# RWKV half pairs of a hybrid step: where the chunk decay is applied, which engine masks and copies, and in which order small products are issued

## The chip, the cores and the metric

The kernel runs on one core of a Trainium2 chip, as one program. A core has five engines that work side by side and wait for each other through semaphores: TensorE (PE in the profile: matrix products into PSUM), VectorE (DVE), ScalarE (ACT), GpSimd (POOL) and SyncE (SP, which issues the DMAs here). PSUM, into which products are written, is used here in eight banks of 512 fp32 columns. The metric is the device time of the execution in microseconds (us); less is better. Three executions of the kernel before took 3572.85, 3575.87 and 3577.72 us.

## The reference

One layer is computed for 512 latent tokens and 128 context tokens with shared weights: an adaLN modulation, one input projection, attention (8 heads) beside a bidirectional RWKV-7 mixer (16 heads of 64), an output projection with a post-norm, and a SwiGLU feed-forward part with a post-norm. The change works on the mixer, and on one small product of attention. The mixer's core is a scan in each direction:

```python
    def step(S, inp):
        r_t, w_t, k_t, v_t, kk_t, a_t = inp
        sa = jnp.einsum("bhvk,bhk->bhv", S, -kk_t)
        S = S * w_t[:, :, None, :] + sa[..., None] * (kk_t * a_t)[:, :, None, :] + v_t[..., None] * k_t[:, :, None, :]
        return S, jnp.einsum("bhvk,bhk->bhv", S, r_t)
```

So a state S of 64 x 64 for each head is decayed by w, corrected along kk, and extended by v k; the output is S r. In attention a score is the product of query and key without position, plus the product of their rotary parts.

## The kernel before

**Tiling.** The 640 tokens lie along the free axis, features on the 128 partitions. Two heads make a pair: head h of a pair stands on partitions 64h to 64h + 63. A pair is worked in two half pairs, j = 0 and 1; in each, the forward direction (d = 0) takes one half of the tokens and the backward direction (d = 1) the other. Tokens go in chunks of 64 (C), five for each direction, so 10 chunks a half pair (NCH), and there are 8 x 2 = 16 half pairs.

**A half pair.** `rwkv_decays` forms decay and learning rate by low-rank products (a full product with the rounded weights, and one with 64 rows for the remainder) and, by a scan, the decay inside each chunk (`dd`, whose last column is kept as `dc`, the decay of the whole chunk). `rwkv_prep` writes the scaled keys `nk` (10 chunks x 128 columns) and the scaled queries `pr`, one tile for each head. `rwkv_grams` forms nk x pr of each chunk and head, a product with 64 rows, 128 output partitions and 128 columns; EG groups the chunks 4, 4 and 2, and each group and head takes one PSUM bank. From the bank ACT copies one part to `mab`, DVE writes one part times a causal mask back into `pr`, and DVE writes the last part times the mask into `mrb`. `inverse` inverts the triangular matrices of all chunks: four copies of `mab` by ACT into a diagonal layout `nd`, a row of small DVE operations, and then products of 32 x 32. Beside it `rwkv_turned` turns values into `sv` (ACT) and `zv` (DVE) and transposes `nk` into `bk`.

**The chain.** `rwkv_chain` then walks the five chunks, both directions and heads together. A step forms x from the state (`m<-sv,pr`, hop "x"), multiplies it by the inverse (`m<-xs,uf`, hop "s") into `zv`, and forms the product pn for the new state (`m<-zv,bk`, hop "y"). On DVE, `sd` = pn + old state, and the new state is `sd` times `dc`. `outputs` adds, for each direction in turn, the state's part (`m<-pr,sv`) and the values' part (`m<-mrb,zv`) of y; both directions share a bank. Then comes hop "p".

**The order of the work.** PE's instructions stand in an order written out when the program is built: class `Jobs` keeps a set of generators with ranks and a planned clock (`Tensor.now`), and always goes on with the ready one of the lowest rank. A generator yields a hop, the planned time in us until it is ready again, from `HOPS` (the first table while the input projection runs, the second while attention does). RWKV has rank 0, its side work (decays of the next half, `rwkv_post`, `rwkv_bonus`) 1, the modulation weights 2, attention 3, the input projection 4. While RWKV waits for a hop, a lower job fills PE. PE then runs the list strictly in order. On the other engines the framework orders the instructions itself, by dependencies and a simulated timeline. It also keeps two engines from reading one PSUM bank at once.

**PSUM.** `mps()` gives one of three banks (tag "m") in turn, to grams, chain, decays, inverse and some of attention; `acc()` gives two tiles of two banks to the projections and scores; `xps()` gives one bank.

**Attention.** Operands are split into a rounded high part and a remainder. `product` sums five products a score; the last has the 64 rows of the head's rotary query part (`qx`) and the rotary key's remainder `krl`. Keys, values and the rotary key parts share 12 slots (`kslot`, N_K).

In the profile the tile names tell these apart: `m<-pr,nk` grams, `m<-xl,lw` the low-rank remainder, `m<-cst,v` the value transposes, `m<-cst,nk` the key transposes, `acc<-krl,qx` the rotary remainder, `acc<-xh,whi` and its like the projections. A form such as 64*128 gives the rows and columns of the array that a product uses. L112 is the line of the helper that issues products, L226 that of the elementwise helper.

## Time and profile before

| what | us |
|---|---|
| median of three executions | 3575.87 |
| the profiled execution, its own time | 3577.47 |
| its span, first to last instruction | 3575.70 |
| start, up to the first half pair's grams | 285 |
| input projection and RWKV | 895 |
| attention and the rest of RWKV | 368 |
| output projection and feed-forward | 2028 |

The stages were told apart by the names of the products that PE runs. The mean granted TensorE clock was 0.959 of full speed. The span is 1.8 us shorter than the execution's own time, which has the launch and the end around it. A row of the order of time gives the start, the time to the end of the last of its instructions, engine, line, operation, tiles, shapes and count; a row of grouped instructions gives busy time and mean, then the engine's idle time just before them and what ended it. [...]

### The profile page before, as it was taken

How to read it: one execution, taken by the hardware profiler on the slowest of the kernel's cores; microseconds unless marked ns; L12 is line 12 of the kernel's file. 1: busy time of each engine (PE TensorE's matmuls, PEld its weight loads, DVE VectorE, ACT ScalarE, POOL GpSimd, SP SyncE). 2: the span in 40 equal slices, each digit the busy share in tenths (PEclk: the TensorE clock that was granted, in tenths of full speed). 3: DMA queues.
4: the chain of work that ended last, by engine and by line, in shares of the span. 5: the costliest groups of instructions: out<-in, count | busy, mean ns of one | idle time of the engine just before them, and what ended most of it. 6: DMA issues, size and time to landing. Idle time of an engine off the chain costs nothing. (4 is left out here: it accounts for less than half of the span.)

```text
span 3575.7 us, 71303 instructions
## 1 busy us (share of the span) xinstructions
PE 3391.9 (95%) x27538; PEld 3032.9 (85%) x27538; DVE 2627.2 (73%) x4721; ACT 1460.2 (41%) x2987; POOL 994.1 (28%) x944
## 2 busy tenths in 40 slices
PE   8979999999999999999979999999999989999987
PEld 4667776777887778889979999999999989999987
DVE  1355676666676776667788988888888868778898
ACT  1143333333444444444453444444444434334334
POOL 0021111111111212111164544444444432222245
PEclk9988999999998999999989999999999999999997
DMA  8653444444112111066534443444433468666743
GB/s 296 236 171 125 142 152 138 155 153 137 60 58 86 37 41 37 18 215 196 154 113 136 165 129 128 133 138 138 136 124 127 143 227 296 234 245 213 257 126 106
DMA packets 289716, 529.05 MB, mean 148 GB/s; under 512 B 31008, under 2 KB 83680, under 8 KB 289376
## 3 DMA queue, kind: packets, MB, share of 16 engines
q1 hardware_dynamic: 289376, 524.49, 44.6%
q8 instruction: 216, 3.54, 0.4%
q14 instruction: 124, 1.02, 0.1%
HBM read 429.65 MB, written 93.09 MB: 146 GB/s over the span
## 5 line engine op out<-in xcount | busy, mean ns | idle before, releaser
L226 DVE TENSOR_TENSOR ql<-raw,qh 128x512 fp32r<-128x512 f32 (+1 forms) x1136 | 932.2, 834 | 282.9 <-ACT qh L1290 270.4
L1290 ACT CAST qh<-raw 128x512 fp32r<-128x512 f32 (+1 forms) x1136 | 661.0, 589 | 880.5 <-PE b L112 658.2
L226 POOL TENSOR_TENSOR raw<-raw,raw 128x512 f32<-128x512 f32 (+1 forms) x288 | 405.6, 1412 | 824.0 <-DVE ql L226 577.7
L112 PE MATMUL b<-t,qh 128*128 128x320 f32 x2816 | 626.9, 310 | 7.9 <-ACT qh L1290 6.8
L112 PE MATMUL b<-op,qh 128*128 128x320 f32 x2464 | 555.0, 318 | 26.0 <-DMA op<-hd 12.7
L112 PEld LDWEIGHTS b<-t,qh 128*128 128x128 f32 x2816 | 473.7, 189 | 9.1 <-ACT qh L1290 7.5
L112 PE MATMUL b<-p,qh 128*128 128x320 f32 x2112 | 468.2, 310 | 0.7 <-ACT qh L1290 0.7
L112 PEld LDWEIGHTS b<-op,qh 128*128 128x128 f32 x2464 | 422.2, 194 | 37.0 <-DMA op<-hd 15.7
L112 PE MATMUL b<-t,ql 128*128 128x320 f32 x1408 | 436.9, 311 | 5.8 <-DVE ql L226 5.8
L112 PE MATMUL b<-op,ql 128*128 128x320 f32 x1232 | 378.0, 319 | 17.0 <-DVE ql L226 17.0
L112 PEld LDWEIGHTS b<-p,qh 128*128 128x128 f32 x2112 | 354.3, 188 | 1.3 <-ACT qh L1290 1.2
L112 PE MATMUL b<-p,ql 128*128 128x320 f32 x1056 | 327.9, 311 | 7.0 <-DVE ql L226 7.0
L112 PEld LDWEIGHTS b<-t,ql 128*128 128x128 f32 x1408 | 265.2, 188 | 8.7 <-DVE ql L226 8.6
L112 PEld LDWEIGHTS b<-op,ql 128*128 128x128 f32 x1232 | 235.2, 194 | 25.4 <-DVE ql L226 25.0
L226 DVE TENSOR_TENSOR raw<-raw,raw 128x512 f32<-128x512 f32 (+1 forms) x288 | 246.4, 866 | 11.5 <-POOL raw L226 5.8
L112 PE MATMUL acc<-xh,whi 128*128 128x320 f32 x928 | 239.7, 341 | 0.3 <-DVE vS L1145 0.2
L112 PE MATMUL acc<-xh,wlo 128*128 128x320 f32 x928 | 235.6, 336 | 0.8 <-DVE wlo L226 0.8
L112 PE MATMUL b<-mh,qh 128*128 128x320 f32 x1024 | 229.6, 313 | 7.0 <-ACT qh L1290 7.0
L112 PE MATMUL acc<-xl,whi 128*128 128x320 f32 x928 | 236.2, 337 | 0.0
L112 PEld LDWEIGHTS b<-p,ql 128*128 128x128 f32 x1056 | 198.9, 188 | 9.4 <-DVE ql L226 9.4
L263 ACT CAST whi<-raw 128x512 fp32r<-128x512 f32 (+1 forms) x156 | 95.0, 609 | 257.1 <-PE acc L112 167.4
L226 DVE TENSOR_TENSOR wlo<-raw,whi 128x512 fp32r<-128x512 f32 (+1 forms) x156 | 107.3, 688 | 111.4 <-ACT whi L263 79.5
(328 smaller groups left out, 5847.5 us busy)
## 6 DMA issues: line engine op xcount, KB each, us to landing
wm<-in_w_mod_dram SPq DMA_DIRECT2D x64, 1024.0 KB, 5.4
op<-hd SPq DMA_DIRECT2D x154, 320.0 KB, 6.0
raw<-in_w_gate_dram SPq DMA_DIRECT2D x188, 256.0 KB, 2.7
raw<-in_w_up_dram SPq DMA_DIRECT2D x188, 256.0 KB, 2.8
raw<-in_w_down_dram SPq DMA_DIRECT2D x224, 192.0 KB, 3.5
raw<-in_w_in_dram SPq DMA_DIRECT2D x132, 256.0 KB, 2.7
wm<-in_w_mod_dram SPq DMA_DIRECT2D x64, 512.0 KB, 6.2
raw<-in_w_out_dram SPq DMA_DIRECT2D x128, 256.0 KB, 3.2
```

The lines of the kernel that those rows point to most:

```text
L112: self.eng.matmul(out, lhsT, rhs, start=start, stop=stop)
L226: eng.tensor_tensor(out=out, in0=x, in1=y, op=op)
L263: A.copy(hi, r)
L1290: A.copy(hi, x)
```

## The change

It does six things.

1. The scaled keys `nk` are multiplied by the decay of the whole chunk (`dc`) on POOL, after the grams and before the transposes into `bk`. The product pn then comes out decayed.
2. The old state's own part, state times `dc`, is formed by POOL at the head of a step. What is left on DVE behind pn is one addition for each head.
3. ACT copies `mrb` out of PSUM without a mask, and POOL masks all of it once per half pair; POOL also copies the values into `zv`, from `sv`. Of the four diagonal copies two go to DVE.
4. Products of one form are issued together: the grams of both heads by turns (two banks), the two full low-rank products and then both remainders, the state's parts of both directions and then the values' parts (two banks).
5. In attention the rotary remainder of the key gets one tile per head parity, zero in the other half, so the last product of a score has 128 rows.
6. The planner counts paired products at half their time, and the hops "inv" and "p" are smaller; hop "dec" and hop "gram" come twice at once instead of one each.

```diff
 RANK_M = 4
 HOPS = ({"load": 3.73, "pow": 3.84, "kk": 1.18, "dec": 0.92, "prep": 1.68, "vr": 2.17, "tv": 0.36, "bk": 0.36, "gram": 0.36,
-         "inv": 14.4, "d32": 1.2, "d32b": 1.92, "d64": 1.44, "d64b": 1.44, "x": 0.48, "s": 0.6, "y": 0.0, "p": 1.06,
+         "inv": 12.0, "d32": 1.2, "d32b": 1.92, "d64": 1.44, "d64b": 1.44, "x": 0.48, "s": 0.6, "y": 0.0, "p": 0.3,
...
         {"load": 3.69, "pow": 2.76, "kk": 0.42, "dec": 0.36, "prep": 3.6, "vr": 1.2, "tv": 0.85, "bk": 0.54, "gram": 0.79,
-         "inv": 16.13, "d32": 1.51, "d32b": 1.96, "d64": 1.3, "d64b": 1.44, "x": 0.61, "s": 0.6, "y": 0.0, "p": 1.08,
+         "inv": 14.0, "d32": 1.51, "d32b": 1.96, "d64": 1.3, "d64b": 1.44, "x": 0.61, "s": 0.6, "y": 0.0, "p": 0.3,
...
     def __init__(self, eng):
         self.eng, self.now = eng, 0.0
-    def matmul(self, out, lhsT, rhs, start, stop):
+    def matmul(self, out, lhsT, rhs, start, stop, share=1.0):
...
             t = 4 * max(n, 16) * (0.25 if m <= 32 and n > 64 else 0.7 if m <= 32 else 0.8 if m <= 64 else 1.0)
-        self.now += t / 2400.0
+        self.now += share * t / 2400.0
         self.eng.matmul(out, lhsT, rhs, start=start, stop=stop)
     def transpose(self, out, x, ident):
...
             co = 32 * (b % 2)
-            A.copy(nd[pr, :].rearrange("p (t c q) -> p c q t", c=16, q=2)[:, :NCH],
-                   mab[pr, :, co: co + 32].rearrange("p c (q t) -> p c q t", q=2))
+            (V.tensor_copy if b % 2 else A.copy)(nd[pr, :].rearrange("p (t c q) -> p c q t", c=16, q=2)[:, :NCH],
+                                                 mab[pr, :, co: co + 32].rearrange("p c (q t) -> p c q t", q=2))
...
             col = 8 * d + i
-            for t, c0, x, r_, b in ((ld, 0, xw, slice(0, 64), w0_h), (ta, 256, xa, slice(64, 128), a0_h)):
-                ps = mps()
-                w = lw[:, c0 + d * P: c0 + d * P + P]
+            both = [(t, lw[:, c0 + d * P: c0 + d * P + P], x, r_, b, mps()) for t, c0, x, r_, b in
+                    ((ld, 0, xw, slice(0, 64), w0_h), (ta, 256, xa, slice(64, 128), a0_h))]
+            for t, w, x, r_, b, ps in both:
                 T.matmul(ps[:, :HN], w, x[:, nat(d, j)], start=True, stop=False)
-                T.matmul(ps[:, :HN], w[r_], xl[r_, nat(d, j)], start=False, stop=True)
+            for t, w, x, r_, b, ps in both:
+                T.matmul(ps[:, :HN], w[r_], xl[r_, nat(d, j)], start=False, stop=True, share=0.5)
+            for t, w, x, r_, b, ps in both:
                 od = t[:, HV[d]] if d == 0 else t[:, HV[d]][:, ::-1]
                 act(od, ps[:, :HN], AF.Tanh, bias=b[:, col: col + 1], scale=0.5)
-                yield HOP["dec"]
+            yield 2 * HOP["dec"]
...
     def rwkv_turned(i, j, sh, u):
         nk, v = u["nk"], sh["v"]
+        nk3 = nk.rearrange("p c b t -> p c (b t)")
+        tt(G, nk3, nk3, u["dc"][:, :NCH].unsqueeze(2).broadcast_to([P, NCH, P]), ALU.mult)
...
                 A.copy(sv_[hrow(h), es, h, :], ch(ps[hrow(h), :HN]))
-                V.tensor_copy(zv[hrow(h), es, h, :], ch(ps[hrow(h), :HN]))
             yield HOP["tv"]
+        for h in range(2):
+            G.tensor_copy(zv[hrow(h), :, h, :], sv_[hrow(h), :, h, :])
...
             es = slice(e0, e0 + n)
-            for h in range(2):
-                ps = mps()
-                for e in range(n):
+            both = [mps(), mps()]
+            for e in range(n):
+                for h, ps in enumerate(both):
                     T.matmul(ps[:, e * P: e * P + P], nk[rows(h), e0 + e].rearrange("p b t -> p (b t)"),
-                             pr[h][rows(h), e0 + e].rearrange("p b t -> p (b t)"), start=True, stop=True)
+                             pr[h][rows(h), e0 + e].rearrange("p b t -> p (b t)"), start=True, stop=True, share=0.5)
+            for h, ps in enumerate(both):
...
                    con("gmask")[rows(q)].unsqueeze(1).broadcast_to([C, n, P]), ALU.mult)
-                tt(V, mrb[rows(h), es], ps4[rows(h), :, 1, :],
-                   con("gmask")[rows(h), C:].unsqueeze(1).broadcast_to([C, n, C]), ALU.mult)
-                yield HOP["gram"]
+                A.copy(mrb[rows(h), es], ps4[rows(h), :, 1, :])
+            yield 2 * HOP["gram"]
+        tt(G, mrb, mrb, con("gmask")[:, C:].unsqueeze(1).broadcast_to([P, NCH, C]), ALU.mult)
     EG = ((0, 4), (4, 4), (8, 2))
...
         def outputs(c):
-            ps = mps()
-            for d in range(2):
-                e = 5 * d + c
-                ms = slice(0, C) if d == 0 else slice(None, None, -1)
+            pss = [mps()[:, :C] for _ in range(2)]
+            ms = (slice(0, C), slice(None, None, -1))
+            for d, ps in enumerate(pss):
                 for h in range(2):
-                    T.matmul(ps[rows(h), cc(d)], sv_[:, e, h, :], pr[h][:, e, 1, :][:, ms], start=True, stop=False)
+                    T.matmul(ps[rows(h)], sv_[:, 5 * d + c, h, :], pr[h][:, 5 * d + c, 1, :][:, ms[d]], start=True, stop=False)
+            for d, ps in enumerate(pss):
                 for h in range(2):
-                    T.matmul(ps[rows(h), cc(d)], zv[rows(h), e, h, :], mrb[rows(h), e, :][:, ms], start=False, stop=True)
+                    T.matmul(ps[rows(h)], zv[rows(h), 5 * d + c, h, :], mrb[rows(h), 5 * d + c, :][:, ms[d]], start=False, stop=True)
...
                 if j == 0:
-                    A.copy(yc, ps[:, cc(d)])
+                    A.copy(yc, pss[d])
                 else:
-                    tt(V, yc, ps[:, cc(d)], yc, ALU.add)
+                    tt(V, yc, pss[d], yc, ALU.add)
         for e in range(5):
             px = mps()
...
             A.copy(xs, px[:, :2 * C])
+            to = [AFTER[j, d][e] for d in range(2)]
+            ds = [d for d in range(2) if to[d]]
+            n = len(ds)
+            es = slice(5 * ds[0] + e, 5 * ds[-1] + e + 1, 5)
+            dv = slice(ds[0] * C, ds[-1] * C + C)
+            sd = rtile("sd", 2 * C, "xs", 2)
+            for h in range(2):
+                rh = rows(h)
+                tt(G, sd[rh, dv].rearrange("p (d v) -> p d v", v=C), sv_[rh, es, h, :],
+                   dc[rh, es].unsqueeze(2).broadcast_to([C, n, C]), ALU.mult)
...
             yield HOP["s"]
-            to = [AFTER[j, d][e] for d in range(2)]
-            ds = [d for d in range(2) if to[d]]
...
                     T.matmul(pn[rows(h), cc(d)], bk[:, 5 * d + e, h, :], zv[:, 5 * d + e, h, :], start=True, stop=True)
-            sd = rtile("sd", 2 * C, "xs", 2)
-            n = len(ds)
             for h in range(2):
                 rh = rows(h)
-                es = slice(5 * ds[0] + e, 5 * ds[-1] + e + 1, 5)
-                dv = slice(ds[0] * C, ds[-1] * C + C)
-                s2 = sd[rh, dv].rearrange("p (d v) -> p d v", v=C)
-                tt(V, s2, pn[rh, dv].rearrange("p (d v) -> p d v", v=C), sv_[rh, es, h, :], ALU.add)
-                dcb = dc[rh, es].unsqueeze(2).broadcast_to([C, n, C])
-                if len(set(to[d] for d in ds)) == 1:
+                if to[ds[0]] == to[ds[-1]]:
...
                         (cy if to[ds[0]] == "carry" else sh["fs"])[rh, dv].rearrange("p (d v) -> p d v", v=C)
-                    tt(V, dst, s2, dcb, ALU.mult)
+                    p_, s_ = (t[rh, dv].rearrange("p (d v) -> p d v", v=C) for t in (pn, sd))
+                    tt(V, dst, p_, s_, ALU.add)
                 else:
-                    for q, d in enumerate(ds):
+                    for d in ds:
                         dst = sv_[rh, 5 * d + e + 1, h, :] if to[d] == "next" else sh["fs"][rh, cc(d)]
-                        tt(V, dst, s2[:, q], dcb[:, q], ALU.mult)
+                        tt(V, dst, pn[rh, cc(d)], sd[rh, cc(d)], ALU.add)
...
         rope(krs)
-        krh, krl = kslot("krh", F32R), kslot("krl", F32R)
+        krh = kslot("krh", F32R)
+        krl = [kslot("krl", F32R) for _ in range(2)]
         A.copy(krh, krs)
-        tt(V, krl, krs, krh.bitcast(F32), ALU.subtract)
+        for h in range(2):
+            G.memset(krl[h][rows(1 - h)].bitcast(F32), 0.0)
+            tt(V, krl[h][rows(h)], krs[rows(h)], krh[rows(h)].bitcast(F32), ALU.subtract)
         del krs
         yield 0.0
...
             heads[hd] = dict(q=q, qx=qx, k=k, vs=vs, vS=vs[hd % 2], out=aslot("att"))
         def product(ps, hd, qs, ks):
-            hh, rr = heads[hd], rows(hd % 2)
+            hh = heads[hd]
             (qh, ql), (kh, kl), qx = hh["q"], hh["k"], hh["qx"][hd % 2]
             for l, r, n in ((qh[:, qs], kh[:, ks], 0), (qh[:, qs], kl[:, ks], 1), (ql[:, qs], kh[:, ks], 2),
-                            (qx[:, qs], krh[:, ks], 3), (qx[rr, qs], krl[rr, ks], 4)):
+                            (qx[:, qs], krh[:, ks], 3), (qx[:, qs], krl[hd % 2][:, ks], 4)):
                 T.matmul(ps, l, r, start=n == 0, stop=n == 4)
         def scores(hd, qb):
```

## The prediction

> **What bounds the kernel now.** I read the page's list of engines first, then the table of windows by stage, then the order of TensorE's instructions inside one pair of heads.

> ```profile
> PE 3391.9 (95%) x27538; PEld 3032.9 (85%) x27538; DVE 2627.2 (73%) x4721; ACT 1460.2 (41%) x2987; POOL 994.1 (28%) x944
> ```

> The table of windows gives start and end, length, then for PE, PEld, DVE, ACT and POOL the busy time with the count, and then PEclk, DMA share and GB/s.

> ```profile
> 285.00:1180.00 895.00, 851.59 (x9684) 672.21 (x9683) 599.52 (x1353) 337.37 (x813) 133.36 (x198) 0.94 0.37 120
> 1180.00:1548.00 368.00, 350.32 (x3692) 285.14 (x3690) 248.71 (x581) 168.40 (x407) 71.85 (x90) 0.98 0.12 35
> 1548.00:3576.00 2028.00, 1942.30 (x12808) 1905.72 (x12808) 1669.75 (x2584) 882.61 (x1628) 765.92 (x600) 0.97 0.52 170
> ```

> The third window (output projection and feed-forward) is not edited. The first two hold the RWKV chain, which has first call on PE; what it leaves free is filled, first by the input projection, then by attention. PE is busy 95% of both (851.59 of 895, 350.32 of 368), so they are bound by PE: microseconds taken from PE's stream there bring the third window forward, as long as the chain doesn't make PE wait instead. The chain may end earlier than attention; then attention has PE alone. DVE stands at 67% and 68%, POOL at 15% and 20%: neither is the bound.

> A busy time on PE doesn't tell what an instruction costs, since matmuls overlap. I take costs from start to next start. One fp32 product shows as two records.

> ```profile
> 701.99 0.42 PE L112 MATMUL m<-xa,lw 128*128 128x320 f32 x1
> 702.33 0.41 PE L112 MATMUL m<-xl,lw 64*128 64x320 f32 x1
> 702.67 0.56 PE L112 MATMUL acc<-xh,whi 128*128 128x320 f32 x2
> 703.06 0.46 PE L112 MATMUL acc<-xl,whi 128*128 128x320 f32 x2
> 703.36 0.46 PE L112 MATMUL acc<-xh,wlo 128*128 128x320 f32 x2
> ...
> 725.73 0.45 PE L112 MATMUL m<-sv,pr 128*64 128x64 f32 x8
> ...
> 728.36 0.45 PE L112 MATMUL m<-zv,bk 128*64 128x64 f32 x8
> 728.64 0.29 PE L112 MATMUL m<-pr,sv 128*64 128x64 f32 x4
> 728.85 0.33 PE L112 MATMUL m<-mrb,zv 64*64 64x64 f32 x4
> 729.12 0.34 PE L112 MATMUL m<-pr,sv 128*64 128x64 f32 x4
> ...
> 729.64 0.57 PE L112 MATMUL acc<-xl,whi 128*128 128x320 f32 x2
> ...
> 731.01 0.45 PE L112 MATMUL m<-sv,pr 128*64 128x64 f32 x8
> ...
> 736.98 1.16 PE L112 MATMUL m<-pr,nk 64*128 64x128 f32 x8
> 738.07 0.56 PE L112 MATMUL acc<-xh,wlo 128*128 128x320 f32 x2
> ...
> 740.72 1.16 PE L112 MATMUL m<-pr,nk 64*128 64x128 f32 x8
> ...
> 746.10 0.71 PE L112 MATMUL m<-pr,nk 64*128 64x128 f32 x4
> 746.74 0.56 PE L112 MATMUL acc<-xl,whi 128*128 128x320 f32 x2
> ...
> 750.06 0.80 PE L112 MATMUL m<-cst,v 64*64 64x64 f32 x20
> 750.79 1.28 PE L112 MATMUL m<-cst,ysq 128*128 128x2 f32 x10
> ...
> 754.42 0.60 PE L116 MATMUL m<-cst,nk 128*128 128x128 f32 x4
> ```

> Two plain pairs stand 0.30 apart (703.06 to 703.36), 0.15 a product of 320 columns; the pair before them, just behind a product of another form, takes 0.39. So a change of the array's form costs some 0.09 on the side of plain products, and more inside the small runs. The kernel has many changes of form, and the change works on these.

> **The change, part by part.** There are 16 half pairs (8 pairs by j = 0, 1), each with five chain steps.

> *Outputs, 80 steps.* From 728.64 the outputs take four runs to 729.64. The last two (729.12 to 729.64) cost 0.52. In the new order d = 0 and 1 share a run, so two changes of form go and four products stay, in longer runs. The ten products at 750.06 take 0.73, with a change of form in it, about 0.05 each when they follow one another: four cost 0.21. Saved 0.52 - 0.21 = 0.31 a step, **25 us**; none if the second pair doesn't overlap.

> *Grams, 48 groups.* Four products take 1.09 (736.98 to 738.07), two take 0.64 (746.10 to 746.74): 0.225 a product and 0.19 a run, and 0.09 on the run before. A half pair has four runs of four and two of two: 4 x 1.09 + 2 x 0.64 + 6 x 0.09 = 6.2 us. New, the heads alternate between rows 0 to 63 and 64 to 127, with a bank each. If both run at once, a half pair takes 2 x 1.09 + 0.64 + 3 x 0.09 = 3.1, which saves 3.1 x 16 = **49 us**. If not, only the 0.28 a run goes: 3 x 0.28 x 16 = 13 us. The nearest row is the run at 750.06, whose products alternate in the same way: at a gram's price (0.11 for 64 columns, and 0.19) ten would take 1.3, and they took 0.73, so two ran at once. They differ in rows and columns of the array, the grams in rows alone, so it is near but not the same. I take 49.

> *What the grams give back.* The bank of the run that starts at 740.72 is read by three instructions in turn:

> ```profile
> 741.91 0.37 ACT L805 COPY mab<-m 64x256 f32<-64x256 f32 x1
> ```
> ```profile
> 742.33 0.69 DVE L226 TENSOR_TENSOR pr<-m,cst 64x512 f32<-64x512 f32 x1
> 743.04 0.42 DVE L226 TENSOR_TENSOR mrb<-m,cst 64x256 f32<-64x256 f32 x1
> ```

> It is free at 743.46, 1.65 us after the run gives PE up (740.72 + 1.09 = 741.81). Now each run takes one of three banks, so a bank has two more runs and the filler between to come free. New, each group takes two, and the second bank of a group is the first of the group before. ACT's mask copy takes the place of the DVE mask, so a bank still needs some 1.65 us, the other bank one more 0.69. The planner puts 2 x 0.36 = 0.72 us between groups: three pairs of filler, 3 x 0.30 + 0.09 = 1.0 us. PE then waits 1.65 - 1.0 = 0.65, with a DVE busy two thirds of the time perhaps 0.9 to 1.3, before each of the second and third group. Behind that product stand all later matmuls, in order. Bounds: nothing, or 2 x 1.3 x 16 = 42 us. I take 0.75 twice, **24 us lost**: the row's wait and a little for DVE's queue. [...] The trace, where one run takes one bank, can't yet show it.

> *Low-rank products, 32 pairs.* At 701.99 a full product and its half of 64 rows take 0.34 each, so both inputs take 1.36. New: 0.15 for the first, 0.34 for the second with the change of form, 0.34 for both halves together: 0.83. Saved 0.53 beside such neighbours; where the half follows at once on a cheaper full product less, 0.38 if the halves don't overlap. I take 0.44, **14 us**.

> *Rotary remainder in attention, 64 halves of scores and 8 prompt products.*

> ```profile
> 1255.54 0.30 PE L112 MATMUL acc<-krh,qx 128*128 128x320 f32 x1
> 1255.77 0.41 PE L112 MATMUL acc<-krl,qx 64*128 64x320 f32 x1
> 1256.11 0.45 PE L112 MATMUL m<-zv,bk 128*64 128x64 f32 x8
> ```

> The two take 0.57; as 128-row products, with zeros in the other half, 0.30. At most 0.27 x 72 = 19 us; where another form follows anyway, as here, part stays, down to 6. I take **16**. The second remainder tile takes one more of the 12 slots that keys and values share, and its POOL memsets come once: 2 us lost (0 to 8).

> *The chain.* DVE's part behind the state product:

> ```profile
> 728.85 0.61 DVE L226 TENSOR_TENSOR sd<-m,sv 64x128 f32<-64x128 f32 x2 [0.88 <-PE m L112]
> 729.50 0.60 DVE L226 TENSOR_TENSOR sv<-sd,dc 64x128 f32<-64x128 f32 x2
> ```

> The new state was ready at 730.10 and asked for at 731.01, 0.9 to spare. Now the first pair alone remains, done at 729.46. PE asks earlier too: 0.31 by shorter outputs and 0.76 by the hop "p" cut from 1.06 to 0.30, about 0.84 on the chip (a filler pair is planned at 0.27 and takes 0.30): at 729.86, 0.4 to spare. DVE's other work will eat that now and then: 0.05 a step, 4 us lost. The decayed old state is POOL's now, two operations of 128 columns a step:

> ```profile
> L226 POOL TENSOR_TENSOR ks<-ks,ta 128x320 f32<-128x320 f32 x16 | 18.8, 1193 | 86.8 <-DVE ta L226 86.8
> L226 POOL TENSOR_TENSOR y<-y,ks 128x640 f32<-128x640 f32 x8 | 12.6, 1575 | 31.5 <-ACT y L238 31.5
> ```

> These make 0.38 us per 320 columns on 0.81, so 0.96 each, 1.9 us a step. Time to hide it: the spare 0.4, then from a step's first product to its state product, 728.36 - 725.73 = 2.63, and that product's 0.28: 3.3. It fits with 1.4 to spare; 2 us lost where POOL is at something else.

> *POOL's other new work* is the decay of 1280 columns of keys (0.81 + 4 x 0.38 = 2.3 us), a mask of 640 (1.6) and two copies of at most 1.6, some 7 us a half pair. The keys are wanted by the transposes, which came 7.7 us behind the grams (746.74 to 754.42): that covers 2.3, and also the mask queued ahead of it behind the last evacuation, 1.65 + 1.6 + 2.3 = 5.6. The rest is wanted behind the inverse, 12 us or more. With the cover gone the wait would be 2 to 5 us a half pair.

> *DVE's relief.*

> ```profile
> L783 DVE COPY zv<-m 64x320 f32<-64x320 f32 x64 | 31.1, 487 | 4.9 <-ACT sv L782 3.5
> L226 DVE TENSOR_TENSOR mrb<-m,cst 64x256 f32<-64x256 f32 x60 | 25.3, 422 | 0.8
> ```

> 31 us of copies and 25 of masks leave DVE, and two of four diagonal copies leave ACT for DVE. DVE isn't the bound; this only pays for the cut of the hop "inv" by 2.4 (31.1 / 16 = 1.9 a half pair, and copies side by side). Counted 0, with 4 us either way.

> *Attention alone* at the end, for some 100 us more, loses a little by its own waits: 3 us.

> **Sum.** Gains 25 + 49 + 14 + 16 = 104. Losses 24 + 2 + 4 + 2 + 3 = 35. Net 69 us. The profiled execution ran 3577.5 us (span 3575.7): 3508. That run is 1.6 us above the median shown, so **3507 us** for the median.

> **The clock** is the term that I can't place. Windows around two drops:

> ```profile
> 475.20:478.60 3.40, 1.61 (x28) 0.95 (x20) 2.80 (x6) 0.00 (x0) 0.17 (x3) 0.99 0.27 96
> 478.60:482.00 3.40, 3.40 (x22) 2.83 (x23) 0.78 (x3) 0.33 (x2) 0.00 (x0) 0.50 0.91 241
> 888.20:891.60 3.40, 3.25 (x26) 2.85 (x24) 2.80 (x7) 0.37 (x1) 0.00 (x0) 1.00 0.43 158
> 891.60:901.80 10.20, 10.20 (x32) 8.08 (x32) 5.04 (x11) 5.80 (x11) 0.00 (x0) 0.50 0.00 0
> ```

> After 1.8 us of waiting the granted clock was 0.50 for 3.4 us; at 888, among grams and with hardly a wait, it fell for 10.2 us. Two new waits a half pair can bring drops, fuller grams can spare some. I set it at 0. [...]

> **Rivals.**

> *A. The banks don't hold PE up* (more filler falls between groups, or the readers come sooner). Then the 24 us stay: 3507 - 24, about 3483. For it: the planner may put a longer run there. Against: three banks for two a group.

> *B. The pairing does nothing for the grams*, since rows alone don't run at once. Grams give 13, low-rank 12: 25 + 13 + 12 + 16 = 66, less about 27 of losses: 3537. Against it stands the row at 750.06.

> *C. Slower: the bank waits bring the half clock.* In each half pair two waits of 1.3 us fall close together behind the grams and the clock halves for 10.2 us as at 891.6, which costs 5.1: 16 x (2.6 + 5.1) = 123 against gains of 104, and 11 of other losses: about 3606. It decides from about 12 half pairs of 16. Against it: now waits of about 1 us mostly pass without a drop, and few of 16 half pairs show a long one.

> *D. No change:* half of the half pairs as in C, with the grams as in B.

> **How the numbers follow.** The forecast 0.52, A 0.18, B 0.14, C 0.08, D 0.08. Faster is the forecast, A and B: 0.84; same 0.08; slower 0.08. A measurement of this kernel tells about 0.2%, 7 us, from no change. The range holds the forecast with its bounds, A and B: below, A with the full low-rank and rotary gains (about 3470) and fewer clock drops, 3455; above, B with 42 instead of 24 for the banks and a few drops, 3562.

> **What would show it.** Right: grams in runs of 16 records of about 1.1 us, outputs in two runs, the remainder as 128-row products 0.15 apart, the output projection starting near 1480 instead of 1548, new idle time before m<-pr,nk ended by ACT or DVE of some 24 us. Wrong: gram runs of 2 us (B), no idle before them (A), a granted clock well under 0.94 in the first window (C), long idle before m<-sv,pr or idle ended by POOL (the chain or POOL's part mis-sized).

## The result, and the profile after

The changed kernel takes **3604.40 us** (median of four executions, 3599.28 to 3609.45) against 3574.36 us before (four, 3571.19 to 3577.72): a ratio of 1.0084, 95% interval 1.0068 to 1.0100. It is slower by 0.8%, clear of no change; 3507 us was forecast. The profiled executions took 3577.47 us before and 3599.28 now, 21.8 us apart, so the profiles show some 8 us less of the loss than the medians.

The page's list of engines, and the table of windows over the same three stages as before (start and end, length, then PE, PEld, DVE, ACT, POOL, then granted clock, DMA share, GB/s):

```profile
PE 3324.2 (92%) x27538; PEld 3001.3 (83%) x27538; DVE 2583.6 (72%) x4434; ACT 1463.2 (41%) x3051; POOL 1154.3 (32%) x1170
```
```profile
285.00:1260.00 975.00, 876.10 (x10797) 693.25 (x10796) 625.75 (x1279) 374.44 (x960) 284.24 (x414) 0.92 0.35 112
1260.00:1568.00 308.00, 265.04 (x2542) 236.76 (x2541) 172.06 (x353) 131.37 (x314) 76.19 (x98) 0.92 0.11 35
1568.00:3597.50 2029.50, 1935.10 (x12808) 1901.11 (x12808) 1671.91 (x2583) 881.75 (x1627) 767.40 (x600) 0.97 0.51 170
```

The last stage kept its length (2028 before, 2029.5 now). The loss lies ahead of it: the output projection starts at 1568.0 instead of 1548.6. Length less busy time gives PE's idle time there: 43.4 + 17.7 = 61 us before, 98.9 + 43.0 = 142 now. The mean granted clock fell from 0.94 and 0.98 to 0.92 in both. PE ran the same 27538 instructions.

From here on one split is used for every run, over the stretch from 255 us to the start of the output projection, counted from the trace's record of each product and of the granted clock: length = PE's idle time + half of the time that PE was busy at granted clock 0.50 (what the half clock cost) + **work**, that is, about what the stretch would last at full clock without waits. Half is a little much: two plain pairs of the changed kernel stand 0.53 apart at a granted clock of 0.51 (624.40 and 624.93), and 0.30 apart at 1.00 (619.35 and 619.65), so 0.43 of that time is lost. With 0.43 the cost below would rise by 26 us instead of 30, and the work fall by 87 instead of 91. The last wait, some 6 us straight before the output projection and alike in all runs, is left in the work.

| | start of output projection | idle | half clock (stretches) | of it with PE busy; its cost | work |
|---|---|---|---|---|---|
| before | 1548.6 | 65 | 142 (15) | 129.5; 64.7 | 1163.7 |
| after | 1568.0 | 146 | 222 (35) | 188.8; 94.4 | 1072.3 |
| difference | +19.4 | +81 | +81 | +59; +30 | -91 |

So most of the savings are there: 91 us of work against 104 forecast. What was mis-sized most is what they gave back: 81 us of waits against 35 of all losses, and 30 us by the clock against 0. The split is good to some 10 us of work: the changed kernel and the runs below that issue its instructions in another order come out between 1054 and 1076.

**The parts, in the order of time** (start, time to the end of the last, engine, line, operation, tiles, shapes, count, and in brackets PE's idle time before it and what ended it). First the savings:

```profile
728.75 0.41 PE L113 MATMUL m<-xw,lw 128*128 128x320 f32 x1
729.00 0.31 PE L113 MATMUL m<-xa,lw 128*128 128x320 f32 x1
729.24 0.41 PE L113 MATMUL m<-xl,lw 64*128 64x320 f32 x2
729.58 0.56 PE L113 MATMUL acc<-xh,whi 128*128 128x320 f32 x2
...
1338.53 0.40 PE L113 MATMUL m<-pr,sv 128*64 128x64 f32 x8
1338.86 0.45 PE L113 MATMUL m<-mrb,zv 64*64 64x64 f32 x8
1339.24 0.56 PE L113 MATMUL acc<-xl,whi 128*128 128x320 f32 x2
...
1360.84 0.31 PE L113 MATMUL acc<-krh,qx 128*128 128x320 f32 x1
1360.98 0.31 PE L113 MATMUL acc<-krl,qx 128*128 128x320 f32 x1
1361.13 0.31 PE L113 MATMUL acc<-kh,qh 128*128 128x320 f32 x1
...
1361.87 0.38 PE L113 MATMUL x<-PT,vS 128*128 128x128 f32 x2
...
1366.73 1.16 PE L113 MATMUL m<-pr,nk 64*128 64x128 f32 x16
1367.82 0.39 PE L113 MATMUL m<-kh,qh 128*128 128x256 f32 x1
```

The low-rank four take 0.83 (728.75 to 729.58), as forecast. The outputs take 0.71 instead of 1.00 (1338.53 to 1339.24; 728.64 to 729.64 before): 0.29 saved against 0.31. The rotary remainder stands 0.15 from its neighbours. A gram group that is not held up runs its eight products (16 records) in 1.09 (1366.73 to 1367.82), as long as four took before: the two heads do run at once.

Then two gram groups and what they wait for, on PE, DVE and ACT:

```profile
617.22 0.49 PE L113 MATMUL m<-pr,nk 64*128 64x128 f32 x2
617.90 1.13 PE L113 MATMUL m<-pr,nk 64*128 64x128 f32 x14 [0.19 <-DVE pr L227]
618.96 0.56 PE L113 MATMUL acc<-xh,wlo 128*128 128x320 f32 x2
619.35 0.46 PE L113 MATMUL acc<-xh,whi 128*128 128x320 f32 x2
619.65 0.45 PE L113 MATMUL acc<-xl,whi 128*128 128x320 f32 x2
620.03 0.49 PE L113 MATMUL m<-pr,nk 64*128 64x128 f32 x2
621.80 1.97 PE L113 MATMUL m<-pr,nk 64*128 64x128 f32 x14 [1.29 <-ACT mrb L818]
```
```profile
618.85 0.89 DVE L236 SCALAR_TENSOR_TENSOR us<-t,mu_h,us 128x641 f32<-128x641 f32 x1
619.77 0.85 DVE L227 TENSOR_TENSOR lw<-raw,lw 64x256 fp32r<-64x256 f32 x2
620.66 1.41 DVE L227 TENSOR_TENSOR pr<-m,cst 64x512 f32<-64x512 f32 x2
```
```profile
618.88 0.76 ACT L814 COPY mab<-m 64x256 f32<-64x256 f32 x2 [2.63 <-PE m L113]
621.38 0.37 ACT L818 COPY mrb<-m 64x256 f32<-64x256 f32 x1 [0.63 <-DVE pr L227]
```

A group that is held up behind its second record takes 0.49 + 1.06 = 1.55 (617.22, and 617.90 to 618.96), and the waiting beside that. The next group's first two records go at once, the third stands until ACT has read `mrb` out of the other bank, at 621.75. The filler between the groups is 1.07 long (618.96 to 620.03), as forecast. But the bank took 621.75 - 618.96 = 2.8 us to come free, not 1.65: DVE was at `us` and `lw`, which belong to a later pair, until 620.62. The granted clock around such waits stands in the table of windows cut at the clock's own steps:

```profile
618.50:621.90 3.40, 2.11 (x19) 1.61 (x15) 3.26 (x6) 1.72 (x4) 1.25 (x4) 1.00 0.91 328
621.90:625.30 3.40, 3.40 (x20) 3.14 (x20) 1.52 (x3) 1.10 (x3) 0.00 (x0) 0.51 0.90 324
625.30:628.70 3.40, 1.88 (x13) 1.35 (x12) 1.06 (x3) 2.15 (x6) 0.32 (x1) 0.99 0.39 119
628.70:632.10 3.40, 3.40 (x17) 1.82 (x15) 3.20 (x5) 2.00 (x4) 2.29 (x2) 0.51 0.00 0
```

Two bank waits in a row, and behind each a window at half clock. Over the stretch, grouped by form (records, busy us and mean ns, idle time before and what ended it), before and after:

```profile
L112 PE MATMUL m<-pr,nk 64*128 64x128 f32 x640 | 104.8, 304 | 9.6 <-DVE nk L226 9.6
L112 PE MATMUL m<-xa,lw 128*128 128x320 f32 x30 | 12.1, 405 | 0.3 <-DVE y L226 0.3
```
```profile
L113 PE MATMUL m<-pr,nk 64*128 64x128 f32 x640 | 76.1, 330 | 51.9 <-DVE nk L227 20.7 <-ACT mrb L818 17.9 <-DVE y L227 8.4
L113 PE MATMUL m<-xa,lw 128*128 128x320 f32 x30 | 11.7, 388 | 9.3 <-DVE y L227 8.7 <-DVE kk L236 0.3 <-ACT ld L239 0.3
```

POOL's new work did not show on PE: no wait of size ends with it. (The one long wait on PE that ends with POOL, 4.2 us before `acc<-cst,P` at 1326.82, is for attention's own softmax tile, which waited for DVE.) The groups on POOL:

```profile
L227 POOL TENSOR_TENSOR sd<-sv,dc 64x128 f32<-64x128 f32 x128 | 61.8, 482 | 239.0 <-DVE sv L227 205.0 <-issue 25.3 <-DVE fs L227 3.9
L227 POOL TENSOR_TENSOR nk<-nk,dc 128x1280 f32<-128x1280 f32 x15 | 35.0, 2330 | 89.4 <-PE m L113 76.0 <-ACT mrb L818 13.2
L227 POOL TENSOR_TENSOR mrb<-mrb,cst 128x640 f32<-128x640 f32 x15 | 24.2, 1612 | 13.4 <-ACT mrb L818 13.4
```

### The profile page after: what moved, and what is told of

Read it like the earlier page. It is cut to its first block, busy times and chain, and to the rows that moved or that the text cites. A ratio compares the mean times of both kernels' runs of the same rounds, so it can differ in the third digit from the quotient of the medians.

```text
span 3597.5 us, 71431 instructions
## 1 busy us (share of the span) xinstructions
PE 3324.2 (92%) x27538; PEld 3001.3 (83%) x27538; DVE 2583.6 (72%) x4434; ACT 1463.2 (41%) x3051; POOL 1154.3 (32%) x1170
## 5 line engine op out<-in xcount | busy, mean ns | idle before, releaser
L227 DVE TENSOR_TENSOR wlo<-raw,whi 128x512 fp32r<-128x512 f32 (+1 forms) x156 | 114.6, 735 | 125.4 <-ACT whi L264 94.8
```

The costliest lines, as they stand in the source:

```text
L227: eng.tensor_tensor(out=out, in0=x, in1=y, op=op)
```

## The experiments

Each run has one profile of its own; idle, half clock with its cost in brackets, and work are the split above, taken from that one execution, which lies up to 9 us from the median. "Alone" is the time from the start of RWKV's last centering product (`m<-y,cst`), when little but attention is left, to the output projection. Ratios are to runs of the kernel before on the same chip.

| kernel | us | ratio [95%] | idle | half clock (cost) | work | alone |
|---|---|---|---|---|---|---|
| before | 3574 | | 65 | 142 (65) | 1164 | 20 |
| after | 3604 | 1.0084 [1.0068, 1.0100] | 146 | 222 (94) | 1072 | 134 |
| before + three regroupings, no grams | 3607 | 1.0085 [1.0057, 1.0113] | 114 | 222 (100) | 1102 | 16 |
| before + low-rank pairs | 3624 | 1.0132 [1.0116, 1.0147] | 99 | 206 (92) | 1145 | 16 |
| before + outputs, remainder | 3551 | 0.9914 [0.9888, 0.9940] | 78 | 155 (71) | 1120 | 19 |
| before + paired grams | 3572 | 0.9995 [0.9980, 1.0010] | 98 | 146 (65) | 1129 | 28 |
| before + engine moves | 3582 | 1.0022 [1.0008, 1.0036] | 74 | 117 (53) | 1164 | 20 |
| before + smaller hops | 3666 | 1.0243 [1.0222, 1.0265] | 105 | 262 (116) | 1161 | 124 |
| after, grams by head | 3615 | 1.0114 [1.0098, 1.0130] | 111 | 269 (121) | 1098 | 112 |
| after, old hops | 3572 | 0.9996 [0.9985, 1.0007] | 141 | 162 (73) | 1073 | 26 |
| after, gram hop 1.6 | 3561 | 0.9969 [0.9959, 0.9979] | 140 | 186 (80) | 1061 | 76 |
| after, gram hop 2.2 | 3555 | 0.9947 [0.9931, 0.9962] | 134 | 170 (71) | 1060 | 28 |
| **after, gram hop 2.4** | **3525** | 0.9867 [0.9852, 0.9882] | 126 | 132 (53) | 1062 | 18 |
| after, gram hop 2.6 | 3558 | 0.9952 [0.9933, 0.9971] | 140 | 162 (69) | 1064 | 15 |
| after, gram hop 3.2 | 3564 | 0.9965 [0.9949, 0.9981] | 136 | 198 (83) | 1054 | 16 |
| 2.4 and old hops | 3589 | 1.0038 [1.0025, 1.0051] | 151 | 220 (89) | 1058 | 17 |
| 2.4 behind two groups | 3581 | 1.0019 [1.0009, 1.0029] | 151 | 192 (83) | 1061 | 56 |
| 2.4, low-rank apart | 3544 | 0.9906 [0.9889, 0.9922] | 119 | 118 (49) | 1080 | 25 |
| after, pair 7 first | 3589 | 1.0044 [1.0029, 1.0059] | 137 | 207 (95) | 1076 | 144 |
| after + discarded products | 3620 | 1.0130 [1.0104, 1.0156] | 150 | 216 (93) | 1092 | 135 |

### One part at a time

**Grams by head again, in the changed kernel.**

```diff
-            both = [mps(), mps()]
-            for e in range(n):
-                for h, ps in enumerate(both):
+            for h in range(2):
+                ps = mps()
+                for e in range(n):
...
-            yield 2 * HOP["gram"]
+                yield HOP["gram"]
```

> The changed kernel with the grams as they were: one head after the other, one PSUM bank a run; all else of the change stays. Theory 1 (the two banks a gram group make PE wait, and the waits bring the half clock): PE's waits before the grams fall from 52 us to about 21 (the first grams and the stage boundary stay), half-clock time falls from 219 us in the two stages to about 160, which gives 30 + 30 us back, and 25 us of faster grams are lost: about 3570 against 3604. Theory 2 (the chain outruns the input projection and is bare at the stage boundary, and attention is left alone): the loss isn't in the grams, so only their 25 us are lost, 3630. Theory 3 (the hops inv and p are cut too far): as theory 2, 3630.

3615 us, between the 3570 and 3630 of its theories. Idle fell by 36 us, so the pairs do bring waits; work rose by 26. But half clock rose by 47 us where theory 1 had it fall, although only one of its stretches, at the start, begins behind a gram's wait now. Undoing the pairs doesn't mend the kernel.

**Paired grams alone, in the kernel before** (the same edit the other way, masks left on DVE).

> The kernel before with paired grams alone, 0.72 us planned behind a group, masks by DVE, hops as before. Theory C: 29 us less work, some 20 us more waits for the banks and 20 to 40 us more half clock (10 to 20 us of time): 3570 to 3590. If pairing hurts only together with the shorter hops: 3545.

3572 us, no change: work -35, idle +33, the half clock's cost 0. The pair is worth 26 to 35 us (from this run and the last), not 49, and here it gives that back in waits.

**The other three regroupings alone, then in two parts.**

```diff
+            both = [(t, lw[:, c0 + d * P: c0 + d * P + P], x, r_, b, mps()) for t, c0, x, r_, b in
...
+            pss = [mps()[:, :C] for _ in range(2)]
...
+        krl = [kslot("krl", F32R) for _ in range(2)]
```

> The kernel before with three of the regroupings alone: both low-rank products together, the outputs of both directions together, the rotary remainder as 128 rows. No paired grams, no work moved between engines, hops as before. Real work on TensorE, counted at full clock, falls by 101 us from before to the changed kernel, 29 of it by the grams, so 72 here. Theory C (the clock halves behind a stretch of 3.4 us in which the array did less than a third of its full work; waits at the grams and a denser chain bring that): nothing here adds waits or density, so waits stay near 65 us and half clock near 142 us, and all 72 come out: 3500 to 3515. Theory M (what hurts is the work moved to POOL and ACT): the same, 3505. Theory O (any faster chain outruns the input projection and pays for it at the boundary): 3545.

> The kernel before with one regrouping alone: the low-rank products in pairs, for which two banks are taken at once; grams, outputs, remainders, engines and hops as before. Its own saving in TensorE's work was forecast at 14 us. Theory L (taking two banks at once behind the feed of the chain is what cost the three regroupings their gain: in that run m<-xa,lw waited 17.4 us for DVE's y, before 0.3): slower than before, 3585 to 3600 us, with 10 to 17 us of waits before m<-xa,lw. Theory P (no part does it; each regrouping shifts where the planned filler falls, and what comes of that, in waits and in half clock, is of either sign): 3560 to 3580, with waits before m<-xa,lw under 6.

> The kernel before with the other two regroupings alone: outputs with both directions in one run and a bank each, and the rotary remainder as 128-row products with a tile for each head; low-rank products as before. Their saving in TensorE's work was forecast at 25 + 16 = 41 us. Theory L (the low-rank pair is what costs): 3530 to 3545 us, with waits and half clock as before (65 and 142 us up to the output projection). Theory P (the shift itself costs, by waits and half clock): 3555 to 3605, with half clock over 170 us.

All three: 3607 us, with 62 us less work; none of its theories had it slower than before. The low-rank pairs alone: 3624 us, with 19 us less work. Outputs and remainder alone: 3551 us, between its two theories; of 44 us of work they keep some 28 on the same chip. So the low-rank pair is what costs in the kernel before. One of its waits, on PE and on DVE, in the order of time:

```profile
1061.56 0.31 PE L113 MATMUL m<-xw,lw 128*128 128x320 f32 x1
1065.05 0.63 PE L113 MATMUL m<-xa,lw 128*128 128x320 f32 x1 [3.17 <-DVE y L227]
```
```profile
1061.61 0.69 DVE L592 TENSOR_REDUCE it<-ip 128x64 f32<-128x512 f32 x1
1062.33 1.27 DVE L231 TENSOR_SCALAR ue<-it,cst 128x256 f32<-128x256 f32 x2
1063.63 1.04 DVE L598 STREAM_TRANSPOSE uc<-ue 128x512 f32<-128x512 f32 x1
1064.53 0.85 DVE L227 TENSOR_TENSOR y<-y,m 128x320 f32<-128x320 f32 x2
```
```profile
1061.00:1064.40 3.40, 0.87 (x6) 0.61 (x4) 3.30 (x5) 0.57 (x1) 1.98 (x3) 1.00 0.19 63
1064.40:1067.80 3.40, 2.75 (x9) 2.20 (x10) 1.39 (x4) 0.94 (x2) 0.00 (x0) 0.51 0.26 99
1067.80:1071.20 3.40, 3.40 (x14) 2.89 (x12) 0.69 (x1) 0.62 (x1) 0.00 (x0) 0.50 0.00 0
```

The second bank of the pair is asked for 0.3 us behind the first. It still holds a product for `y`, whose reader on DVE is queued behind the inverse's own steps. PE waits 3.17 us and runs the next two windows at half clock. In the kernel before, the same place looks so:

```profile
1055.88 0.31 PE L112 MATMUL m<-xw,lw 128*128 128x320 f32 x1
1056.12 0.41 PE L112 MATMUL m<-xl,lw 64*128 64x320 f32 x1
1056.46 0.56 PE L112 MATMUL acc<-xh,wlo 128*128 128x320 f32 x2
...
1057.75 0.31 PE L112 MATMUL m<-xa,lw 128*128 128x320 f32 x1
```

There 1.3 us of filler (1056.46 to 1057.75) stood between the two requests, and this wait came to 0.3 us in the whole run.

**The engine moves alone** (the changed kernel with the regroupings and hops of before).

> The changed kernel with every regrouping undone and the old hops: what is left is the work moved between engines (decay in the keys and state's own part by POOL, masks of mrb by ACT and POOL, value copies by POOL, two diagonal copies by DVE). Theory C: nothing on TensorE changes, 3572 within 8. Theory M: the loss is here, 3600 or more.

3582 us, +0.2%: work 1164, as before, idle +8, half clock -25. What DVE gave to POOL and ACT neither costs nor brings much, as forecast.

**The smaller hops alone, and the old hops put back.**

```diff
-         "inv": 14.4, "d32": 1.2, ... "p": 1.06,
+         "inv": 12.0, "d32": 1.2, ... "p": 0.3,
...
-         "inv": 16.13, "d32": 1.51, ... "p": 1.08,
+         "inv": 14.0, "d32": 1.51, ... "p": 0.3,
```

> The kernel before with the smaller hops alone (inv 12.0 and 14.0, p 0.3): the same instructions, the chain's parts asked for earlier, less filler put between them. Theory H (the cut of the hops costs by itself, as putting them back into the changed kernel gave 32 us): 3590 to 3605 us, with longer waits before m<-sv,pr, m<-pm,uc or m<-pr,sv. Rival (the cut costs only beside the other parts of the change, where the chain catches up with the input projection): 3565 to 3580. Where no instruction is changed, any difference is the order's alone.

> The changed kernel with the hops inv and p of before (14.4 and 16.13 us, 1.06 and 1.08 us). Theory 3: waits for the inverse, for the chain and for the decays (some 25 us with their half clock) go: about 3575. Theory 1: the gram waits stay, 3600. Theory 2: the chain is some 90 us longer, so the bare stretch at the stage boundary shrinks: 3590.

In the kernel before, the smaller hops cost most of all parts, 87 us, without one instruction changed and beyond both of its theories: idle +40, and half clock +120, which costs 51. The waits that grew do not lie where theory H looked for them but at the head of the inverse (the group of that run; m<-tc,mab had 5.3 before):

```profile
L112 PE MATMUL m<-tc,mab 32*32 32x32 f32 x1280 | 16.8, 211 | 48.3 <-DVE tc L599 48.2
```

PE asks for the inverse before DVE has its diagonal blocks, in 15 waits of 3.2 us on average. Eleven stretches of half clock, 119 us, begin right behind these waits. In the changed kernel, where DVE has fewer copies ahead, this wait is 9.3; there the old hops gain 32 us, most of it by half clock (222 to 162, 22 us of cost), 6 by waits.

### The filler behind the grams

```diff
-            yield 2 * HOP["gram"]
+            yield 2.4
```

(1.6, 2.2, 2.6 and 3.2 alike; in the changed kernel it is 0.72 beside the input projection and 1.58 beside attention.)

> The changed kernel with paired grams, but 2.4 us of planned filler behind each group instead of 0.72. Theory 1: the banks are free when the next group comes; the grams' waits fall by about 25 us and the half clock by about 50 us (25 us of time), pairing is kept: about 3555. Theory 2: the chain gets 16 x 5 us longer and outruns the projection less, a little better, 3595. Theory 3: no change, 3604.

> The changed kernel with 1.6 us planned behind each gram group (0.72 beside the input projection and 1.58 beside attention in the changed kernel, 2.4 in the run at 3525 us). Theory G (filler behind the groups covers the bank waits): half of the gain of 2.4, 3555 to 3575 us, with 8 to 14 us of waits before m<-pr,nk that end with ACT's mrb (18.1 without, 3.6 with 2.4). Theory O (any shift of the plan deals waits and half clock anew): anywhere from 3510 to 3620, and the wait before m<-pr,nk says nothing of the time.

> The changed kernel with 3.2 us planned behind each gram group. Theory G: the waits that end with ACT's mrb are gone (under 2 us), but they were 3.6 already; the chain gets longer by up to 48 x 0.8 = 38 us, and it ended 18 us ahead of the output projection with 2.4, so it becomes the bound: 3530 to 3550 us. Theory O: anywhere from 3510 to 3620.

> The changed kernel with 2.2 us planned behind each gram group. Balance: between the runs with 1.6 (3561) and 2.4 (3525) on a straight line 3534, so 3525 to 3543 us, attention alone at the end for 18 to 40 us. Order (each shift deals waits and half clock anew, and 2.4 was a lucky deal): over 3545 us, with half clock over 165 us up to the output projection (131 with 2.4).

> The changed kernel with 2.6 us planned behind each gram group. Balance: between the runs with 2.4 (3525) and 3.2 (3564) on a straight line 3535, so 3525 to 3545 us, and no long stretch of half clock at the end of the chain or one under 25 us. Order: over 3547 us, or under 3515, with half clock that has no place of its own.

With 2.4 the changed kernel takes 3525 us, the fastest of all versions, and the nearest to the forecast. From 1.6 on, the waits that end with ACT's `mrb` fall from 18 us to 8, 8, 4, 3 and 1, and all five values gain 40 us or more. But the curve is no smooth bottom: 3561, 3555, 3525, 3558, 3564. Both neighbours of 2.4 lie where their expectations put the cause down to the order. So some 40 to 49 us come with enough filler behind the groups; the last 30 belong to one order of the products that 0.2 us more or less does not give.

At 3.2 the other end shows. The table of windows of that run, near the chain's end:

```profile
1440.00:1453.00 13.00, 10.59 (x142) 8.49 (x140) 6.93 (x15) 4.42 (x20) 6.15 (x10) 1.00 0.00 1
1470.00:1521.00 51.00, 32.89 (x496) 26.48 (x494) 20.34 (x59) 9.06 (x24) 7.25 (x14) 0.57 0.01 3
```

No `acc` product is among the 496 of the last row: attention's filler is used up, the chain is alone, and 51 us pass at a clock of 0.57. In the changed kernel as it is, attention is left alone for 134 us instead.

> The changed kernel with 2.4 us behind each gram group and the old hops (inv 14.4 and 16.13, p 1.06 and 1.08). Theory G (the filler is spent evenly only while chain and filler end together): the chain, 18 us ahead at 2.4, gets longer by some 80 us, as it did when the old hops were put back alone, and sets the end: 3570 to 3595 us, with little half clock and attention starved of nothing but time. Rival (the cut of the hops is a cost in itself, 32 us as the run with old hops showed): 3485 to 3500.

> The changed kernel with 2.4 us behind the first and the second gram group alone, and the changed kernel's own hop (0.72 or 1.58) behind the third, where no group waits for a bank. Theory G: as fast as with 2.4 behind all three, 3515 to 3535 us, and waits before m<-pr,nk ended by ACT's mrb of some 4 us. Theory O: 3545 to 3610, with such waits gone all the same.

> The changed kernel with 2.4 us planned behind each gram group, as in the run at 3525 us, and the low-rank products taken apart again (one bank at a time, as before). Theory L (the pair's two banks cost more than the pair saves): 3500 to 3515 us, waits before m<-xa,lw under 3 us (10.5 in the run with 2.4 alone). Theory P: the 10 to 14 us of saved work come back, 3530 to 3545; a larger difference of either sign would be the order's.

More filler does not go on helping: with the old hops as well, 3589 us. Theory G had that time, but with little half clock, and it was not little: 220 us, again with long stretches at the end (two of 44 us from 1452 on), when the filler has run out. Taking the hop away behind the third group, where no bank is waited for, should have cost nothing and cost 55 us, spread over many small waits (151 us idle) and half clock: theory G fell. Its waits for `mrb` stayed at 4 us, so the bank waits alone don't set the time. So did theory L for the low-rank pair apart (theory P's 3530 to 3545 held): its wait goes (10.5 to 0.8 us), but some 19 us of work come back, and 3544 is slower than 3525. The pair costs 45 us in one order and pays in another.

### Two that settled little

```diff
-ATT_POS = 23
+ATT_POS = 26
```

> The changed kernel with ATT_POS 26: the input projection makes the last pair's tiles before attention's inputs, so the last pair needn't wait for them. Theory 2: the bare stretch from 1235 to 1290 us goes (19 us of waits and 17 us by the half clock, against about 20 in the kernel before): about 3585. Theories 1 and 3: the loss stays where it is, 3600.

3589 us. In the changed kernel the chain catches up with the input projection: once, PE waits bare for the last pair's keys.

```profile
1259.83 1.66 PE L113 MATMUL m<-krs,rot 128*128 128x512 f32 x2 [1.21 <-ACT ta L239]
1273.18 2.08 PE L113 MATMUL m<-pr,nk 64*128 64x128 f32 x10 [11.69 <-DVE nk L227]
```

With attention's place in the order moved, that wait is gone (the gram waits that end with `nk` fall from 20.9 to 9.1 us), but the other gram waits rise by 8, and the whole gains 15 us.

```diff
             both = [mps(), mps()]
+            for _ in range(5 if e0 else 0):
+                T.matmul(both[0][:, :HN], xw[:, :P], xw[:, :HN], start=True, stop=True, share=0.0)
```

> The changed kernel with five full products of 320 columns ahead of the second and third gram group, written to the bank that the group then overwrites: 0.74 us of work that is thrown away, 24 us in all, in the place where TensorE waits for a bank. The planned order is otherwise the same. Theory C: the array's share in those stretches rises past a third, the half clock falls from 222 us to about 160 (30 us of time) and the waits by about 18, while 24 us are added: about 3580 against 3604. If the clock doesn't follow the array's work: the waits fall by 18 and 24 are added, 3610.

3620 us: work +20, idle +4, half clock -6. The waits for `mrb` fell by 8 us and others rose by 12. The half clock did not fall to 160 us, and 12 of its stretches (75 us) still begin behind a gram's wait. Filling waits with empty products does not pay here, and the run does not show that more work in the array would have kept the clock up.

## Why the prediction was wrong

Point by point:

- **The savings: near in sum.** 91 us of work against 104. Outputs and remainder 44 against 41 (alone), low-rank 19 against 14, grams 26 to 35 against 49, the one term that was clearly too large. The two heads do run at once (1.09 us for eight products), but where a bank is late the group is cut behind its second record and runs 1.55; the row at 750.06, taken as the nearest, has no such stop.
- **What the grams give back: right mechanism, a size that was near by luck.** 24 us were forecast. Waits before the grams rose by 42: 18 for ACT's `mrb`, 8 for banks that `y` still holds, 3 for `pr`, 2 for ACT's `us`, and 11 for the keys, nearly all at the one place at 1273. The forecast had a wait of 0.75 at each of 32 places. The bank waits, for `mrb` and `y`, were 18, of 1.5 us on average: fewer, and longer where they came (1.29 in the rows above), where the bank takes 2.8 us to come free, since its DVE reader stands behind other DVE work.
- **The failed step: "I set it at 0", the clock, and with it the other waits.** Idle rose by another 39 us before other products, at some fifteen groups of them (9 before m<-xa,lw, 8 before x<-cst,ev, 6 before acc<-cst,P, 4 before m<-tc,mab, and so on). Low-rank pairs and outputs too take two of the three banks at once, and the forecast charged that to the grams alone. The smaller hop "inv" was counted at 0 on DVE's relief and "p" at next to nothing; beside that relief putting both back gains 32 us, and without it they cost 87. And half clock came with the waits: 142 to 222 us, 30 us lost. Of the 35 stretches of half clock, 12 (72 us) begin behind a gram's wait. The row at 475.20 had shown a drop behind 1.8 us of waiting (there for the chain's `zv`, not for a bank).
- **POOL, DVE's relief, the chain: right, or on the safe side.** `sd` takes 0.48 us for 128 columns (0.96 forecast), the keys 2.33 (2.3), the mask 1.61 (1.6), and PE waits nowhere for them.
- **The rivals.** C gave 3606 us, and 16 x 7.7 = 123 us of waits and half clock; 81 + 30 = 111 came. It had them all behind the grams, where about half of the waits and a third of the half clock lay, so that its time comes this near is partly luck. It had a chance of 0.08. The trace has 35 stretches of half clock instead of 15, but 23 of the 35 do not begin behind a gram's wait.

What stays open: what makes one order of the same products 30 us better than its neighbours (2.2, 2.4 and 2.6 us behind the grams). The split tells where the time lies in each (idle 126 to 140, half clock 132 to 170), not what would give the better order on purpose. The parts don't add up either: what a part costs or gains, the low-rank pair and the hops above all, depends on the order that the others leave.

## What to carry to other kernels

Where PE's order is planned to hide everything else, work saved on PE is also cover taken away (here 91 us of work went and 81 us of waits came): price every saving together with the waits that its microseconds hid, above all where a regrouping takes two PSUM banks at once and the banks' readers share a queue with other work. Re-plan the filler after such a change and time several values, since the order alone moved this kernel by 30 to 90 us, as much as the whole gain. And count half clock as a cost: beside the waits it rose here from 142 to 222 us, and cost 26 to 30 us.

## What the hardware showed that was not expected

| work as a share of a full-clock window | windows | next one at 0.50 |
|---|---|---|
| under 0.25 | 250 | 249 |
| 0.25 to 0.36 | 263 | 189 |
| 0.36 to 0.45 | 386 | 75 |
| 0.45 and over | 5651 | 1 |

In half clock, with the share taken of half a window's capacity, the next window was at full clock in 273 of 274 cases from 0.9 on, in 191 of 305 from 0.7 to 0.9, and in 50 of 518 below 0.7. PE's busy time did not tell the same: of the full-clock windows with PE busy for 90% and more but a share under 0.36, 17 of 39 were followed by half clock; of those with PE busy for less than 60% but a share of 0.45 and over, none of 30. The drop at 888.20 in the forecast, which had hardly a wait, fits: PE was busy 3.25 of 3.40 us, but with products of 64 rows, and the share comes to 0.32. It is a regularity over the runs; no run changed the share alone, and the discarded products, which were to raise it behind the grams, left the half clock where it was.

The windows at 618.50 and 625.30 above, with PE busy for 2.11 and 1.88 of 3.40 us, were each followed by one at half clock.
